# Splitting layer 2's k, r, v and LoRA weights during layer 1, and mixing block 0's operands twice

## The chip, the cores and the metric

The kernel runs on 1 core of one Trainium2 chip. The metric is the device time of one execution in microseconds (us). A profile of one execution shows what every engine did: TensorE (PE in the rows, PEld for its weight loads), VectorE (DVE), ScalarE (ACT), GpSimd (POOL), SyncE (SP, whose queue issues nearly all DMAs), and the 16 DMA engines.

## The reference

A trunk of four layers works on 256 context tokens and 1024 image tokens of width 1024, in float32. Layers 0 and 3 are RG-LRU mixers, layer 1 is an mLSTM mixer, layer 2 an RWKV-7 mixer. Cut to what matters here:

```python
# layer 1, mLSTM: 8 heads, q and k of 128, v and z of 256 columns a head
q, k, v, z, g = jnp.split(h @ w_in, splits, axis=-1)
# a recurrence over chunks, in both directions; then
out = (norm(hsum) * norm_g * silu(z)) @ w_out

# layer 2, RWKV-7: every projection has an operand of its own, mixed with the shifted tokens
xs = h[None] + (shifted - h)[None] * mu[:, None, None, :]        # r, k, v, z, w, a
r, k, v, z = einsum('gbtd,gde->gbte', xs[:4], w_rkvz)
w_pre = w0 + tanh(xs[4] @ w1) @ w2                               # LoRA of rank 64, two directions
a = sigmoid(a0 + (xs[5] @ a1) @ a2)                              # LoRA of rank 64, two directions
# then a recurrence over the tokens, forwards and backwards, for 16 heads
```

## The kernel before

Matrix products are done in three passes: weight and operand are each split into a rounded high part and the low part that remains, and high x high, high x low and low x high are added up (`mm3`, L107). So each weight is loaded raw, its high part is a cast, and its low part a subtraction.

**How instructions get their order.** Outside layer 2's scan the builder orders each engine's instructions by readiness in program order of priority. A tile of a pool gets one of the pool's buffers (their number is given for each name) once an earlier tile has been let go. `issue_after(x)` puts the instructions of x's engine that are made inside it behind x.

**Layer 1** (`mlstm`, L604) runs eight heads. Each head makes, in program order, q and k (three chunks of tokens each, `proj`), v (ten chunks, L650 to L652), the gate matrices E and Q for both directions, the products q k (L671), and then a loop of ten steps, in each step both directions (L678 to L711): the numerator (L689, L691), a normalisation by its last column (L693 to L695), the weighted keys on GpSimd (L703), the outer product (L705) and the new state on DVE (L83, from L710). Behind the loop come z0 and z1 (L714), the group norm and the output. Steps 1 to 6 also contain `ahead(1)`, one portion of the modulation parameters of layers 2 and 3, which DVE computes from loaded rows (`mw`, L230 and L232).

All weights of layer 1 come through `weight` (L96): the load at L101 on SP, the cast at L103 on DVE, the low part at L88 on GpSimd. Its tiles `wraw`, `whi` and `wlo` of 128x1024 come from the pool `wt`, which has two buffers for each name (L59).

**Layer 2** (`rwkv_scan`, L793) works on five blocks of 256 tokens, in the groups G0 = block 0, G1 = blocks 1 and 4, G2 = blocks 2 and 3. `stream` (L959) runs a list of projections: pieces of weights of 128x512 are loaded raw (`load`, at most two), split (`split`, cast on ACT at L986, low part on GpSimd, or on DVE in the first part) and, but for the two LoRA projections, written to memory in two parts (L992), so that later groups load the parts alone (L979, at most three pairs of buffers). `mixed` (L846) makes a projection's operand from h: a scaling on ACT, a shifted multiply-add on DVE, the high part on ACT, the low part on GpSimd or DVE. The first list is

```python
group(G0, (4, 5) + krv, half), group(G0, krv, rest, True), group(G1, (4, 5) + krv), ...
```

(4 and 5 are the LoRA projections, `krv` is k, r, v; `half` and `rest` are the first and the last four column tiles.) In the first group of G0 the operands of k, r and v are also written to memory (L897) and in the second they are read back (`again`, L903). The list's first 120 units run alone, up to r of the first group; the rest is dealt out between the instructions of the scan, whose order on each compute engine is the written one. The scan's first recurrence matmul (L1411) runs at 2143.8 us.

Of the kernel before, what the change touches and what calls it, by code (L numbers as in the profile page):

```python
# [10 lines left out]
F32 = mybir.dt.float32  # L11
# [19 lines left out]
class Net:  # L31
    def __init__(self, ctx, tc, aps):
        self.tc, self.nc, self.ctx = tc, tc.nc, ctx
        self.a = aps
        nc = self.nc
        pool = lambda name, bufs, **k: ctx.enter_context(tc.tile_pool(name=name, bufs=bufs, **k))
        self.const = pool("const", 1)
        self.sm = pool("sm", 1)
        self.base = ExitStack()
        self.open_base()  # L40
        c = self.const
        self.ones = c.tile([128, 128], F32, name="ones")
        nc.gpsimd.memset(self.ones, 1.0)
        self.ident = c.tile([128, 128], F32, name="ident")
        nc.gpsimd.affine_select(
            out=self.ident, in_=self.ones, pattern=[[-1, 128]], compare_op=ALU.is_equal,
            fill=0.0, base=0, channel_multiplier=1,
        )
        self.mhalf = c.tile([128, 16], F32, name="mhalf")
        nc.gpsimd.memset(self.mhalf, -0.5)  # L50
        self.vecs = c.tile([128, aps["vecs"].shape[1]], F32, name="vecs")
        nc.sync.dma_start(out=self.vecs, in_=aps["vecs"])
        self.spill = {}
        self.last = None

    def open_base(self):
# [547 lines left out]
    def mlstm(self, l, hs):  # L604
        nc = self.nc
# [3 lines left out]
        with ExitStack() as es:  # L609
# [6 lines left out]
            bc = lambda t: t.unsqueeze(2).to_broadcast([128, 10, 128])  # L616
            order = (tuple(range(10)), (1, 0) + tuple(range(9, 1, -1)))
            groups = ((0, 2), (2, 4), (6, 4))
            gof = {c: gi for gi, (a, n) in enumerate(groups) for c in range(a, a + n)}
            for h in range(8):  # L620
                E, Q = [], []
                w = self.weight(self.a["mlstm_w_q"][h], 8)
# [4 lines left out]
                w = self.weight(self.a["mlstm_w_k"][h], 8)  # L627
# [16 lines left out]
                for c in range(10):  # L644
                    ps = self.pm.tile([128, 512], F32, tag="pm", name="pm")[:, 0:256]
                    t = slice(c * 128, (c + 1) * 128)
# [7 lines left out]
                for d in (0, 1):  # L654
                    e = self.w(n=T, name="E")
# [11 lines left out]
                for gi, (a, n) in enumerate(groups):  # L667
                    ps = self.pa.tile([128, 512], F32, tag="pa", name="pa")
                    for i in range(n):
                        t = slice((a + i) * 128, (a + i + 1) * 128)  # L670
                        mm(ps[:, i * 128:(i + 1) * 128], kT[:, t], qT[:, t], start=True, stop=True)  # L671
                    for d in (0, 1):
                        p = E[d][:, a * 128:(a + n) * 128]
# [4 lines left out]
                for i in range(10):  # L678
                    for d in (0, 1):
                        if d and 0 < i < 7:  # L680
                            self.ahead(1)
                        c = order[d][i]
                        t = slice(c * 128, (c + 1) * 128)
                        gi = gof[c]
# [28 lines left out]
                for j in (0, 1):  # L713
                    w = self.weight(self.a["mlstm_w_z"][2 * h + j], 8)  # L714
# [15 lines left out]
                for a, n in groups:  # L730
                    for j in (0, 1):
# [6 lines left out]
                        self.stt(V, y[:, 0:n * 128], ps[:, 0:n * 128], ng[:, 2 * h + j:2 * h + j + 1], zs[j][:, s], ALU.mult, ALU.mult)  # L738
                        nc.sync.dma_start(out=yd[2 * h + j][:, s], in_=y[:, 0:n * 128])
            self.ahead(96)  # L740
        return yd

    def rwkv(self, l):
        hd = self.dram("r7h", (8, 128, T))
# [45 lines left out]
    def rwkv_scan(self, es, hd, zd, yd, xd):  # L792
# [46 lines left out]
        def parts(k, n):  # L839

            if n > 256 or k % 2 == 0:
                held[0] = tile_("xh", [128, 512], F32R, 8), tile_("xl", [128, 512], F32R, 8)
            o = 256 * (k % 2) if n == 256 else 0
            return [t[:, o:o + n] for t in held[0]]

        def mixed(g, k, blks, xs):  # L846
# [43 lines left out]
            S.copy(out=hi[:, 0:n], in_=t[:, 0:n])  # L890
            yield
            self.lo(V if early and k % 2 else G, lo[:, 0:n], t[:, 0:n], hi[:, 0:n])
            if g < 3 and blks == (0,):
                if k == 0:
                    xsp[g, blks] = [self.dram(f"r7x{g}_{blks[0]}_{j}", (2, 128, n)) for j in range(8)]
                for j, x in enumerate((hi, lo)):
                    nc.sync.dma_start(out=xsp[g, blks][k][j], in_=x.bitcast(F32))  # L897

        def again(g, k, blks, xs):

            xs[k] = parts(k, 256 * len(blks))
            for j, x in enumerate(xs[k]):
                nc.sync.dma_start(out=x.bitcast(F32), in_=xsp[g, blks][k][j])  # L903
            yield

        def drain(*gens):
            for g in gens:
# [46 lines left out]
                    done(c, acc[c])  # L954
            return job, [(name + (k,), w_ap[:, k * 512:k * 512 + 512]) for k in range(8)], 1, steps, 6

        wsp, xsp = {}, {}

        def stream(passes):  # L959

# [21 lines left out]
            def split():  # L982
                name, raw = raws.pop(0)
                hi, lo = pair()
                ready.append(((hi, lo), g))
                S.copy(out=hi, in_=raw)  # L986
                yield
                self.lo(V if early else G, lo, raw, hi)
                if name[0] != "l1":
                    d = self.dram("r7s" + "_".join(map(str, name)), (2, 128, 512))  # L990
                    for j, t in enumerate((hi, lo)):
                        nc.sync.dma_start(out=d[j], in_=t.bitcast(F32))  # L992
                    wsp[name] = d

            def start(gen):
                if gen is not None and next(gen, 0) is None:
# [42 lines left out]
                ready.pop(0)  # L1039
            drain(*work)  # L1040

        def group(blks, what, es=range(8), kept=False):
            n = 256 * len(blks)
            for g in what:
                job = Job(blks, [lambda xs, g=g, k=k, f=again if kept else mixed: f(g, k, blks, xs) for k in range(8)])
                if g >= 4:
                    def done(ps, g=g):
                        t = tile_("po", [128, 512], bufs=3)
# [447 lines left out]
        for k in range(8):  # L1496
# [2 lines left out]
        half, rest = range(4), range(4, 8)  # L1499
        krv = (1, 0, 2)  # L1500
        first = stream(itertools.chain(
            group(G0, (4, 5) + krv, half), group(G0, krv, rest, True), group(G1, (4, 5) + krv), group(G2, (4, 5) + krv),
            *(group(g, (3,)) for g in (G0, G1, G2)), output(G0, range(8), self.xsrc)))

        n = 120
# [220 lines left out]
```

## Time and profile before

| | us |
|---|---|
| median of 3 runs | 4512.19 |
| lowest and highest | 4493.22, 4515.55 |
| the profiled execution | 4495.78 |
| its span, first to last instruction | 4493.2 |

By stages of the profiled execution: layer 1's heads lie from about 690 to 1640 us, the first weight load of layer 2 is at 1912.9, the first matmul of its scan at 2143.8 and the last at 3875.8. In the rows a line can be that of a helper: L88 and L83 are the helpers for two-operand and three-operand instructions, so the names of the tiles tell more. A landing is the time from the issue of a DMA to its end.

### The profile page before, as it was taken

To read this page: it belongs to the slowest core of one execution; us is meant where nothing else is said; L and a number is where in the kernel's file an instruction comes from. 1 tells how busy PE (TensorE), PEld (TensorE's weight loads), DVE (VectorE), ACT (ScalarE), POOL (GpSimd) and SP (SyncE) were. 2 spreads that over 40 slices of the span, in tenths; PEclk is the share of its full clock that TensorE was granted. 3 is DMA by queue.
4 is the path that set the end of the run, shared out by engine and by line. 5 is a ranking of instruction groups with operands and counts; after the bars stand their busy time and mean duration, and the time that the engine had idled before them with its cause. 6 is when DMAs were issued, how large, how long until landed. Compare 5 with 4: busy or idle time off the path is not lost. (4 is left out here: it accounts for less than half of the span.)

```text
span 4493.2 us, 113560 instructions
## 1 busy us (share of the span) xinstructions
PE 3909.5 (87%) x47428; PEld 3173.9 (71%) x47428; DVE 2738.5 (61%) x5032; ACT 1960.7 (44%) x4103; POOL 2024.7 (45%) x1867
## 2 busy tenths in 40 slices
PE   5999898999999979857898799888888878779978
PEld 3677777888889868745676576666666766557766
DVE  4477746445555562444667666566688777467884
ACT  4577513222222220244544555455444544267760
POOL 2466623333333342125544533444455755347662
PEclk9999998999999989877999899988989879889999
DMA  5311422222222242388445645655344645411132
GB/s 210 121 47 51 151 86 71 88 92 92 92 88 91 88 163 65 118 297 275 147 145 172 195 162 163 208 153 163 111 127 134 208 129 156 155 60 54 52 114 81
DMA packets 355072, 581.10 MB, mean 129 GB/s; under 512 B 59232, under 2 KB 197472, under 8 KB 354432
## 3 DMA queue, kind: packets, MB, share of 16 engines
q1 hardware_dynamic: 354560, 573.85, 39.2%
q8 instruction: 373, 6.11, 0.6%
q14 instruction: 139, 1.14, 0.1%
HBM read 434.60 MB, written 139.10 MB: 128 GB/s over the span
## 5 line engine op out<-in xcount | busy, mean ns | idle before, releaser
L88 POOL TENSOR_TENSOR wlo<-wraw,whi 128x512 fp32r<-128x512 f32 (+3 forms) x260 | 483.6, 1861 | 752.5 <-DVE whi L103 375.0
L113 PE MATMUL pm<-hlo,whi 128*128 128x512 f32 (+1 forms) x1648 | 614.9, 373 | 10.0 <-DVE hlo L83 10.0
L114 PE MATMUL pm<-hhi,wlo 128*128 128x512 f32 (+1 forms) x1648 | 605.2, 370 | 11.8 <-POOL wlo L88 11.8
L112 PE MATMUL pm<-hhi,whi 128*128 128x512 f32 (+1 forms) x1648 | 612.0, 372 | 0.6 <-ACT hhi L290 0.6
L112 PE MATMUL pz<-xh,whi 128*128 128x512 f32 (+1 forms) x784 | 362.4, 463 | 27.4 <-DMA wraw<-in_r_l 17.4
L114 PEld LDWEIGHTS pm<-hhi,wlo 128*128 128x128 f32 x1648 | 312.5, 190 | 64.9 <-POOL wlo L88 15.2
L113 PEld LDWEIGHTS pm<-hlo,whi 128*128 128x128 f32 x1648 | 312.7, 190 | 63.8 <-DVE hlo L83 11.4
L112 PEld LDWEIGHTS pm<-hhi,whi 128*128 128x128 f32 x1648 | 313.3, 190 | 54.0 <-issue 1.7
L112 PE MATMUL pm<-yhi,whi 128*128 128x512 f32 (+1 forms) x816 | 302.9, 375 | 51.5 <-DVE x L83 28.2
L114 PE MATMUL pz<-xh,wlo 128*128 128x512 f32 (+1 forms) x784 | 302.8, 386 | 23.5 <-POOL wlo L88 23.2
L113 PE MATMUL pm<-ylo,whi 128*128 128x512 f32 (+1 forms) x816 | 303.6, 373 | 4.4 <-DVE ylo L88 2.5
L113 PE MATMUL pz<-xl,whi 128*128 128x512 f32 (+1 forms) x784 | 303.2, 387 | 2.0 <-POOL xl L88 1.0
L114 PE MATMUL pm<-yhi,wlo 128*128 128x512 f32 (+1 forms) x816 | 298.5, 373 | 4.0 <-POOL wlo L88 4.0
L88 POOL TENSOR_TENSOR t<-t,kin 128x256 f32<-128x256 f32 x88 | 82.4, 936 | 375.2 <-DVE t L1210 341.2
L103 DVE CAST whi<-wraw 128x1024 fp32r<-128x1024 f32 (+4 forms) x129 | 94.5, 733 | 257.4 <-PE pm L652 149.7
L83 DVE SCALAR_TENSOR_TENSOR x<-pm,mod,x 128x512 f32<-128x512 f32 (+1 forms) x208 | 136.5, 665 | 183.3 <-PE pm L114 165.8
L88 POOL TENSOR_TENSOR O<-DG,lev 128x256 f32<-128x256 f32 x200 | 160.4, 810 | 177.2 <-issue 117.7
L88 POOL TENSOR_TENSOR xl<-mx,xh 128x512 fp32r<-128x512 f32 (+1 forms) x146 | 178.5, 1232 | 130.0 <-ACT xh L890 85.8
L112 PEld LDWEIGHTS pm<-yhi,whi 128*128 128x128 f32 x816 | 156.1, 192 | 85.2 <-DVE x L83 31.5
L112 PEld LDWEIGHTS pz<-xh,whi 128*128 128x128 f32 x784 | 164.7, 210 | 68.4 <-ACT whi L986 27.5
L703 POOL TENSOR_SCALAR kw<-kt,tkwgt 128x128 f32<-128x128 f32 x144 | 105.3, 734 | 233.3 <-PE pa L705 188.9
L83 DVE SCALAR_TENSOR_TENSOR uf<-us,vecs,uf 128x1283 f32<-128x1283 f32 x60 | 158.5, 2641 | 82.8 <-ACT uf L411 80.3
(345 smaller groups left out, 10429.7 us busy)
## 6 DMA issues: line engine op xcount, KB each, us to landing
kin<-r7krk SPq DMA_DIRECT2D x72, 384.0 KB, 3.8
mw<-in_mod_w SPq DMA_DIRECT2D x48, 512.0 KB, 7.6
mw<-in_mod_w SPq DMA_DIRECT2D x96, 256.0 KB, 2.6
wlo<-r7sw SPq DMA_DIRECT2D x96, 256.0 KB, 3.0
whi<-r7sw SPq DMA_DIRECT2D x96, 256.0 KB, 2.7
wraw<-in_lru_w_in SPq DMA_DIRECT2D x40, 512.0 KB, 3.5
UZ<-r7v SPq DMA_DIRECT2D x160, 128.0 KB, 3.3
x<-x SPq DMA_DIRECT2D x28, 640.0 KB, 6.0
```

What stands on the lines that cost most here:

```text
L83: i = eng.scalar_tensor_tensor(out=out, in0=in0, scalar=scalar, in1=in1, op0=op0, op1=op1, **k)
L88: eng.tensor_tensor(out=out, in0=a, in1=b, op=op)
L103: (cast or nc.vector.tensor_copy)(out=hi, in_=raw)
L112: mm(out, w[0][:, c], x[0][:, a:a + b], start=first, stop=False)
L113: mm(out, w[0][:, c], x[1][:, a:a + b], start=False, stop=False)
L114: mm(out, w[1][:, c], x[0][:, a:a + b], start=False, stop=last)
L703: G.tensor_scalar(out=kw, in0=kt[:, t], scalar1=gt["wgt"][:, c, d, h:h + 1], scalar2=None, op0=ALU.mult)
```

## The change

While layer 1 runs, a generator `keep` takes the two LoRA weights, the k and r weights and the v weights of layer 2 in 26 tiles of 128x1024, splits each with `weight`, and writes the parts to memory in pieces of 128x512, under the names that `stream` uses. Its portions stand in the step loop: in the first two heads in steps 1, 3, 4 and 6, in the others in steps 1, 3 and 5, each with its DVE instruction behind the last state update. `stream` starts with these pieces as known ones, so it loads their parts and splits only z's and the output's weights. Block 0's operands of k, r and v are no longer written and read back; the second group of G0 mixes them again from h.

```diff
+            keep = self.keep()
...
                         if d and 0 < i < 7:
                             self.ahead(1)
+                        if d and i in ((1, 3, 4, 6) if h < 2 else (1, 3, 5)):
+                            with self.tc.issue_after(self.last.ins):
+                                next(keep, 0)
...
+    def keep(self):
+        nc = self.nc
+        for j, ap in [(("l1", 4 + g), self.a["r7_l1"][g]) for g in (0, 1)] + \
+                [(("w", g, e), self.a["r7_w"][g, e]) for h in (0, 4) for g in (1, 0) for e in range(h, h + 4)] + \
+                [(("v", h, 2 * k), self.a["r7_wv"][h][:, k * 1024:(k + 1) * 1024]) for h in (0, 1) for k in range(4)]:
+            hi, lo = self.weight(ap, 8)
+            for i in (0, 1):
+                name = (j[0], j[1], j[2] + i) if j[0] == "v" else j + (4 * i,)
+                d = self.dram("r7s" + "_".join(map(str, name)), (2, 128, 512))
+                for p, t in enumerate((hi, lo)):
+                    nc.sync.dma_start(out=d[p], in_=t[:, i * 512:(i + 1) * 512].bitcast(F32))
+                self.kept[name] = d
+            yield 1
...
             self.lo(V if early and k % 2 else G, lo[:, 0:n], t[:, 0:n], hi[:, 0:n])
-            if g < 3 and blks == (0,):
-                if k == 0:
-                    xsp[g, blks] = [self.dram(f"r7x{g}_{blks[0]}_{j}", (2, 128, n)) for j in range(8)]
-                for j, x in enumerate((hi, lo)):
-                    nc.sync.dma_start(out=xsp[g, blks][k][j], in_=x.bitcast(F32))
-
-        def again(g, k, blks, xs):
...
-        wsp, xsp = {}, {}
+        wsp = self.kept
...
-                if name[0] != "l1":
-                    d = self.dram("r7s" + "_".join(map(str, name)), (2, 128, 512))
-                    for j, t in enumerate((hi, lo)):
-                        nc.sync.dma_start(out=d[j], in_=t.bitcast(F32))
-                    wsp[name] = d
+                d = self.dram("r7s" + "_".join(map(str, name)), (2, 128, 512))
+                for j, t in enumerate((hi, lo)):
+                    nc.sync.dma_start(out=d[j], in_=t.bitcast(F32))
+                wsp[name] = d
...
-            group(G0, (4, 5) + krv, half), group(G0, krv, rest, True), group(G1, (4, 5) + krv), group(G2, (4, 5) + krv),
+            group(G0, (4, 5) + krv, half), group(G0, krv, rest), group(G1, (4, 5) + krv), group(G2, (4, 5) + krv),
```

## Rows read from the trace of the kernel before

**Rows 1.** The page: busy time of each engine, share of the span, instructions.
```profile
PE 3909.5 (87%) x47428; PEld 3173.9 (71%) x47428; DVE 2738.5 (61%) x5032; ACT 1960.7 (44%) x4103; POOL 2024.7 (45%) x1867
```

**Rows 2.** Busy time by stretch: start:end, length, each engine busy (instructions), PE clock, DMA share, GB/s.
```profile
1001.40:1064.20 62.80, 62.80 (x305) 53.60 (x304) 43.63 (x140) 13.52 (x40) 16.61 (x17) 1.00 0.27 84
1064.20:1115.40 51.20, 51.20 (x389) 48.86 (x388) 14.38 (x30) 15.45 (x31) 22.15 (x14) 1.00 0.28 99
1115.40:1560.00 444.60, 444.60 (x2664) 398.26 (x2663) 229.11 (x668) 114.39 (x280) 152.67 (x123) 1.00 0.28 93
1912.00:1992.00 80.00, 47.17 (x254) 42.96 (x254) 47.61 (x96) 46.26 (x113) 19.74 (x26) 0.75 0.86 287
1992.00:2144.00 152.00, 106.91 (x1030) 81.89 (x1030) 54.93 (x93) 62.24 (x131) 87.17 (x81) 0.76 0.86 278
```

**Rows 3.** Timeline of TensorE in layer 1, one recurrence step: start, length, instruction.
```profile
1008.83 0.59 PE L689 MATMUL pa<-vt,E 128*128 128x257 f32 x2
1009.26 0.60 PE L691 MATMUL pa<-st,Q 128*128 128x257 f32 x2
1009.69 0.60 PE L705 MATMUL pa<-vt,kw 128*128 128x257 f32 x2
```

**Rows 4.** Timeline of SP's queue in the same head of layer 1: weight loads.
```profile
1001.28 0.33 SPq L101 DMA_DIRECT2D wraw<-in_mlstm_w_q  x1
...
1029.53 0.38 SPq L101 DMA_DIRECT2D wraw<-in_mlstm_w_v  x1
...
1071.93 0.33 SPq L101 DMA_DIRECT2D wraw<-in_mlstm_w_z  x1
```

**Rows 5.** Timeline of DVE, same head: state update, first direction, steps 3, 4, 5.
```profile
1022.97 0.48 DVE L83 SCALAR_TENSOR_TENSOR st<-st,dec,pa 128x257 f32<-128x257 f32 x1
...
1030.60 0.47 DVE L83 SCALAR_TENSOR_TENSOR st<-st,dec,pa 128x257 f32<-128x257 f32 x1
...
1035.82 0.48 DVE L83 SCALAR_TENSOR_TENSOR st<-st,dec,pa 128x257 f32<-128x257 f32 x1
```

**Rows 6.** Busy time of the engines from the recurrence's start to step 3.
```profile
1001.40:1023.00 21.60, 21.60 (x105) 18.38 (x104) 15.19 (x51) 6.15 (x16) 6.17 (x7) 1.00 0.29 86
```

**Rows 7.** The raw weight tiles in layer 1: ns min/median/max, first and last start, forms.
```profile
L103 DVE CAST whi<-wraw x48: 284/694/2314, 642.4 to 1540.1; 128x1024 fp32r<-128x1024 f32 x46, 128x384 fp32r<-128x384 f32 x1, 128x256 fp32r<-128x256 f32 x1
...
L88 POOL TENSOR_TENSOR wlo<-wraw,whi x48: 737/2384/2414, 642.9 to 1540.9; 128x1024 fp32r<-128x1024 f32 x46, 128x384 fp32r<-128x384 f32 x1, 128x256 fp32r<-128x256 f32 x1
...
DMA to landing us min/median/max: 3.3/4.1/8.4
```

**Rows 8.** The loads of z's weights in layer 1.
```profile
DMA to landing us min/median/max: 3.4/7.0/8.4
```

**Rows 9.** Timeline of all engines in layer 1, around one low part on GpSimd.
```profile
1024.09 0.69 DVE L232 SCALAR_TENSOR_TENSOR mw<-mw,scr 128x512 f32<-128x512 f32 x1
...
1026.15 2.37 POOL L88 TENSOR_TENSOR wlo<-wraw,whi 128x1024 fp32r<-128x1024 f32 x1 [2.52 <-PE pa L691]
...
1026.26 2.81 DVE L232 SCALAR_TENSOR_TENSOR mw<-mw,scr 128x512 f32<-128x512 f32 x1
```

**Rows 10.** DMA issues, front of layer 2: xcount, KB each, median us to landing.
```profile
DMA packets 51277, 65.17 MB, mean 281 GB/s; under 512 B 9471, under 2 KB 31161, under 8 KB 51257
...
wraw<-in_r_w SPq DMA_DIRECT2D x32, 256.0 KB, 3.7
...
r7sw<-whi SPq DMA_DIRECT2D x32, 256.0 KB, 4.2
...
xh<-r7x SPq DMA_DIRECT2D x24, 128.0 KB, 4.0
```

**Rows 11.** Groups on ACT, front of layer 2: busy us, mean ns, idle before.
```profile
L986 ACT CAST whi<-wraw 128x512 fp32r<-128x512 f32 x55 | 33.8, 614 | 69.4 <-DMA wraw<-in_r_w 28.0 <-DMA wraw<-in_r_wv 19.3 <-PE pz L113 8.3
...
L868 ACT ACTIVATE mx<-X,omu 128x256 f32<-128x256 f32 x40 | 18.7, 503 | 8.5 <-DMA X<-r7h 6.2 <-POOL xl L88 2.0 <-DVE xl L88 0.2
```

**Rows 12.** Waits of TensorE, front of layer 2: total us, times, longest.
```profile
PE pz L1116 <- ACT kq L1110: 34.5, 8, 8.3
```

More of the change, by code (lines that the diff above doesn't have):

```diff
@@ L52, in __init__ @@
         nc.sync.dma_start(out=self.vecs, in_=aps["vecs"])
-        self.spill = {}
+        self.spill, self.kept = {}, {}
         self.last = None
@@ L740, in mlstm @@
             self.ahead(96)
-        return yd
+            for _ in keep:
+                pass
+        return yd
+    def keep(self):
[11 more added lines that the diff above has]
+            yield 1
     def rwkv(self, l):
@@ L892, in mixed @@
             self.lo(V if early and k % 2 else G, lo[:, 0:n], t[:, 0:n], hi[:, 0:n])
-            if g < 3 and blks == (0,):
-                if k == 0:
-                    xsp[g, blks] = [self.dram(f"r7x{g}_{blks[0]}_{j}", (2, 128, n)) for j in range(8)]
-                for j, x in enumerate((hi, lo)):
-                    nc.sync.dma_start(out=xsp[g, blks][k][j], in_=x.bitcast(F32))
-        def again(g, k, blks, xs):
[L901 to L904, printed above, removed]
         def drain(*gens):
@@ L1040, in stream, with group @@
             drain(*work)
-        def group(blks, what, es=range(8), kept=False):
+        def group(blks, what, es=range(8)):
             n = 256 * len(blks)
             for g in what:
-                job = Job(blks, [lambda xs, g=g, k=k, f=again if kept else mixed: f(g, k, blks, xs) for k in range(8)])
+                job = Job(blks, [lambda xs, g=g, k=k: mixed(g, k, blks, xs) for k in range(8)])
                 if g >= 4:
```

## The prediction

> **What bounds the kernel now.** I read the page's first lines, then the busy time by stretch, then inside two stretches the matmul groups, the issues on SP's queue and the steps on DVE. TensorE is busy for 87% of the span [rows 1], but this hides two very different stages. In layer 1 TensorE has no idle time at all: 62.80 of 62.80 us, 51.20 of 51.20 and 444.60 of 444.60, at a granted clock of 1.00, with the DMA engines at 0.27 to 0.28 [rows 2]. At the front of layer 2, from 1912 to 2144, it is busy 47.17 of 80.00 and 106.91 of 152.00 us at a clock of 0.75 and 0.76, and the DMA engines are at 0.86 in both [rows 2]. So layer 1 pays for whatever takes matmuls from TensorE, and the front of layer 2 pays for bytes. The change moves work from the second to the first.
>
> A layer 1 head takes 114.0 us (62.8 + 51.2). Its recurrence, ten steps in each direction, lies in the 62.8 us [rows 2]. Its own matmuls are short: three kinds in a row start 0.43 us apart [rows 3], and there are 20 + 18 + 18 of them by the code (the first step has no state to read), so 24 us, 2.4 a step. The other 39 us of TensorE are projections with weights already on the chip: z of this head, then q of the next. This filler is why TensorE never waits for the recurrence, whose pace DVE and the hand-overs between engines set.
>
> **Part 1: what the kept weights do to layer 1.** The code gives all weights of layer 1 one pool of two buffers each for the raw tile, the high and the low part, and keep() takes its tiles from that pool. SP's queue shows that buffers are taken in program order, as soon as they are free: q at 1001.28, v at 1029.53, z at 1071.93, the last 43 us before its matmuls, which begin with the next recurrence at 1115.4 [rows 2, 4]. In the code the new tiles stand in the recurrence, after v and ahead of z. Their loads wait for nothing but a buffer, so they come first. Their casts are tied behind the recurrence's update of step 1, 3, 5 (for the first two heads 1, 3, 4, 6). So z0 gets its raw buffer only when the kept tile of step 3 has been split (of step 4 in the first two heads), and z1 that of the one after. Until then TensorE has only the recurrence's 2.4 us a step.
>
> How long: the recurrence of the head shown starts at 1001.4; the update of step 3 in the first direction runs at 1022.97, that is +21.6 us [rows 5]. Without z beside it this can be earlier. DVE was busy 15.19 us up to there [rows 6]; without z's two evictions (an estimate: 0.7 each, as the 0.69 us instructions of their size [rows 9]), and with the first kept tile's cast and its delay (2.8 us, below), that makes +16.6. I take +20, as the DVE work is most but not all of it. Then four 0.69 us instructions of the modulation (2.8 us [rows 9], 3.1 with their read-outs), the cast 0.69 and the low part 2.38 us [rows 7]: the raw buffer is free at +26. The load lands 4.1 us later (3.3 to 8.4 [rows 7]; z's own 7.0 [rows 8]), cast and a place in DVE's order take 1.5: z0's first matmul at +32. A step takes 6.4 us here (1022.97 to 1035.82 for two [rows 5]), so 5 steps, 12 us of matmuls, are done by then: TensorE idles 20 us a head. Ends: the kept tile before the modulation at +16.6, landing in 3.3: +24, 10 us done, 14 us idle; step 3 at +21.6, delays of 2.1 us twice, landing in 7.0: +41, 14.5 us done, 26 us idle. In the first two heads step 4 is 6 to 8 us later (1030.60 [rows 5]), 2.4 us more done: +3.5 idle. Nothing gives it back, as the rest of the head is 51.20 of 51.20 us busy [rows 2]. Eight heads: 8 x 20 + 2 x 3.5 = **+167 us** (119 to 215).
>
> The rest of part 1 costs little by itself. 26 kept tiles are 26 casts at 0.69 (18 us of DVE), 26 low parts at 2.38 (62 us of GpSimd) and 26 x 1.57 MB (512 KB read, four writes of 256 KB) = 41 MB over some 920 us, 44 GB/s beside the stage's 84 to 99, with DMA at 0.27 [rows 2]. DVE has 43.6 of 62.8 us in use in the recurrence [rows 2], GpSimd 16.6. SP's queue takes 26 x 5 issues of 0.33 us; the writes wait there for their cast and low part, and the modulation's loads queue behind them, which is inside the upper end. The cover for all of this is the filler that part 1 takes away.
>
> One thing more lengthens the steps: a low part on GpSimd from 1026.15 for 2.37 us has beside it a modulation instruction on DVE that takes 2.81 us instead of 0.69, and the DVE one ends 0.55 us after it [rows 9]. So each kept tile can hold DVE for 2.1 us; that is the delay above. The Trainium skill, SBUF — State Buffer, section "Who interferes with whom", says that a DVE instruction with two SBUF inputs and a GpSimd instruction that reads SBUF share a port pair, and that the later one waits for the whole of the earlier. The trace agrees with this (2.81 against 0.69 us). By that rule all 26 low parts could hit, 26 x 2.1 = 55 us of DVE; without it the sum would lose some 2 us a head. It speaks against putting this work beside the recurrence.
>
> **Part 2: the front of layer 2.** From 1912 to 2144 the core moves 65.17 MB at 281 GB/s [rows 10]. All 52 weight pieces of the first pass (4 LoRA, 32 of k and r, 16 of v) are loaded raw, 256 KB, and 48 are written back as two parts; 24 operand tiles are written and read back as two parts of 128 KB [rows 10]. Before: 13.6 + 25.2 + 12.6 = 51.4 MB. After: 52 x 512 KB = 27.3 MB, and 24 reads of 128 KB of h for the second mixing, 3.1 MB: 30.4. So 21.0 MB fewer, at 281 GB/s **-75 us**. TensorE's own busy time in this stretch is 154 of 232 us, so 78 is the most while its clock stays at 0.75; where both rise it can be 100. The low end, 55, is where loads in three buffers or the start of the scan set the pace: a pair must be read whole before its first matmul.
>
> ACT loses 52 casts at 0.614 (32 us) and gets 48 instructions for the second mixing, at most 0.503 each (24 us) [rows 11]; it is at 46.26 of 80.00 and 62.24 of 152.00 [rows 2], so it does not become the bound. GpSimd and DVE lose 52 low parts of 512 columns and get 24 of 256, and DVE 24 shifts: less for both. SP issues 52 + 96 + 96 fewer and 104 + 24 more. Later passes read the LoRA weights instead of splitting them: a few microseconds, taken as zero, since TensorE is the fuller engine there. The scan's order is written out, so an earlier start moves its end one for one.
>
> **Sum.** 4495.8 (the profiled execution; span 4493.2) + 167 - 75 = 4588. The ends: +119 - 100 = +19 and +215 - 55 = +160, so 4515 to 4656. The median of the runs shown is 4512.2, 16 above the profiled one; the forecast is on the profiled one's scale.
>
> **Rivals.** *Faster: TensorE keeps its filler.* If z's loads get buffers ahead of the kept ones, or other matmuls are put into the hole, part 1 costs nearly nothing and the time is 4496 - 75 = 4421. For it: the builder orders instructions by readiness, as filler between steps shows; against: every load of [rows 4] is in program order, and q, k and v of the next head stand behind z in the same buffers. It decides for faster where z0's first matmul comes before about +15 us in the step loop, as 75 us over eight heads is 9.4 us idle a head. *No change: half the hole.* If without filler the steps run at twice the pace, the kept tile of step 3 comes at about +11 and z0 at +21, idle 10 us a head: 4496 + 84 - 75 = 4505. For it: TensorE would answer each step at once; against: DVE's 15.19 us [rows 6], of which z's evictions are the small part. *Slower still: part 2 gives little.* If the first pass is held by latency (TensorE waits 34.5 us of it for the tile of the norm of k, a chain of hand-overs [rows 12]), it gives 25: 4496 + 167 - 25 = 4638. That kept weights are not found under their names, and split again, I exclude: the names in keep() are those that stream() asks for; it would be 4663.
>
> **How the numbers follow.** Forecast 0.53, slower still 0.12, no change 0.15, faster 0.20. A measurement of this kernel tells about 0.5% (22 us) from no change. The forecast's low tail and the rival give same 0.15; slower is 0.65, faster 0.20. The forecast's own range is 4515 to 4656; the range given reaches down to 4440 to take in no change and the weak end of the faster case, and ends at 4655, the forecast's own upper end.
>
> **What would show it.** In layer 1: raw loads in the order v, kept, kept, kept, z, and TensorE idle some 20 us in the first half of each recurrence, ended by DVE's cast or GpSimd's low part of z; a head of 130 to 137 us instead of 114.0; perhaps a clock below 1.00 in the hole. In layer 2: some 44 MB from the first weight load to the first chain matmul, in some 157 us instead of 232. Wrong would be: heads of 114 to 118 us, or z loaded before the kept tiles.

## The result and the profile after

The changed kernel takes 4567.66 us (median of 4 runs, 4552.67 to 4570.89), the kernel before 4503.92 (median of 4, 4493.22 to 4515.55) beside it: a ratio of 1.0133, 95% interval 1.0107 to 1.0158. It is slower by 1.3%, as forecast in sign (4588, range 4440 to 4655). Both of the prediction's terms, however, came out about half as large as they were put, and because they have opposite signs their errors partly cancelled: that the total lies near the forecast is in part luck. The profiled executions, 4495.78 before and 4552.67 after, split like this (the scan's row ends with its last output product, 4 us behind the last recurrence matmul):

| stage | before | after | difference | forecast |
|---|---|---|---|---|
| up to layer 1's output (first write of h for layer 2) | 1885.3 | 1979.2 | +93.9 | +167 |
| from there to the first load of h | 23.0 | 22.8 | -0.1 | 0 |
| front of layer 2: first load of h to first scan matmul | 235.5 | 200.6 | -34.9 | -75 |
| scan | 1736.1 | 1737.5 | +1.4 | 0 |
| rest | 613.3 | 610.7 | -2.6 | 0 |
| span | 4493.2 | 4551.0 | +57.8 | +92 |

The engines' busy line of the page of after answers [rows 1]. It tells little, as it did before: TensorE's share falls by one point.

```profile
PE 3934.0 (86%) x47428; PEld 3170.1 (70%) x47428; DVE 2803.2 (62%) x5061; ACT 1942.4 (43%) x4091; POOL 2079.8 (46%) x1878
```

The busy time by stretch tells more. Columns as in [rows 2]; the first two lines are the third head of layer 1, cut 1.8 to 2.2 us ahead of its recurrence as there, the third is four heads, the fourth the whole front of layer 2.

```profile
1030.50:1093.30 62.80, 53.98 (x246) 42.91 (x245) 54.79 (x158) 12.62 (x41) 29.75 (x21) 0.97 0.45 151
1093.30:1157.60 64.30, 64.30 (x448) 59.72 (x447) 11.87 (x13) 15.83 (x32) 20.25 (x13) 1.00 0.24 86
1157.60:1669.60 512.00, 477.07 (x2762) 414.90 (x2762) 265.67 (x681) 114.10 (x284) 199.02 (x136) 0.97 0.34 118
2002.10:2202.70 200.60, 136.16 (x1283) 113.44 (x1283) 98.44 (x190) 97.74 (x237) 79.60 (x97) 0.81 0.73 230
```

The recurrence's stretch, full before, has 8.82 us without a matmul and a clock of 0.97, and DVE is busy 54.79 of its 62.80 us (43.63 before). The front is shorter, at a DMA share of 0.73 instead of 0.85.

**The hole, read instruction by instruction.** SP's queue of the same head, weight loads, answers [rows 4]: the second and third kept tile (named `in_r_w`; the first was loaded at 990.41), and only then z0 and z1.

```profile
1005.44 0.33 SPq L101 DMA_DIRECT2D wraw<-in_r_w  x1
...
1043.62 0.42 SPq L101 DMA_DIRECT2D wraw<-in_r_w  x1
...
1053.96 0.42 SPq L101 DMA_DIRECT2D wraw<-in_mlstm_w_z  x1
...
1062.76 0.42 SPq L101 DMA_DIRECT2D wraw<-in_mlstm_w_z  x1
```

The timeline of all engines in that head shows what z0 waited for.

```profile
1036.40 0.48 DVE L83 SCALAR_TENSOR_TENSOR st<-st,dec,pa 128x257 f32<-128x257 f32 x1
...
1037.41 0.69 DVE L103 CAST whi<-wraw 128x1024 fp32r<-128x1024 f32 x1
...
1038.20 0.68 DVE L232 SCALAR_TENSOR_TENSOR mw<-mw,scr 128x512 f32<-128x512 f32 x1
...
1038.54 2.54 POOL L88 TENSOR_TENSOR wlo<-wraw,whi 128x1024 fp32r<-128x1024 f32 x1
...
1038.81 2.82 DVE L232 SCALAR_TENSOR_TENSOR junk<-mw,scr 128x512 f32<-128x512 f32 x1
...
1047.64 0.46 DVE L83 SCALAR_TENSOR_TENSOR st<-st,dec,pa 128x257 f32<-128x257 f32 x1
...
1048.02 0.68 DVE L103 CAST whi<-wraw 128x1024 fp32r<-128x1024 f32 x1
...
1048.79 2.72 POOL L88 TENSOR_TENSOR wlo<-wraw,whi 128x1024 fp32r<-128x1024 f32 x1 [0.80 <-DVE whi L103]
...
1056.01 0.47 DVE L83 SCALAR_TENSOR_TENSOR st<-st,dec,pa 128x257 f32<-128x257 f32 x1
...
1060.94 0.68 DVE L103 CAST whi<-wraw 128x1024 fp32r<-128x1024 f32 x1
...
1062.35 0.46 DVE L83 SCALAR_TENSOR_TENSOR st<-st,dec,pa 128x257 f32<-128x257 f32 x1
...
1062.35 0.58 PE L112 MATMUL pm<-hhi,whi 128*128 128x512 f32 x1
```

The cast at 1037.41 is the first kept tile's, the one at 1048.02 the second's, right behind the update it is tied to. The second's low part ends at 1051.51, z0's load is issued into that buffer at 1053.96, z0 is cast at 1060.94 (the third kept tile's cast, at 1056.40, is not shown), and its first matmul runs at 1062.35, 31.9 us after the stretch began and 29.7 after the recurrence's first matmul. Until then TensorE has only the recurrence.

The waits of TensorE in the front of after (us in total, times, longest) answer [rows 12].

```profile
PE pz L1124 <- ACT kq L1118: 25.7, 6, 6.8
PE pz L112 <- DMA whi<-r7sl: 16.3, 1, 16.3
PE px L1191 <- DVE bon L1312: 5.9, 1, 5.9
PE pz L112 <- DMA whi<-r7sw: 4.7, 5, 1.8
```

The longest is still the norm of k (34.5 us before, 25.7 now). It makes three tiles, a square, a broadcast factor and the product, one after the other in a single buffer (`kq`), and TensorE's sum over the squares (L1124) waits until ACT has written the square there (L1118), which needs the buffer free. But for the stage's first load, 16.3 us, waits for the weights are small.

### The profile page after: what moved, and what is told of

It is laid out like the page before. It is cut to its first block, busy times and chain, and to the rows that moved or that the text cites. A ratio compares the mean times of both kernels' runs of the same rounds, so it can differ in the third digit from the quotient of the medians.

```text
span 4551.0 us, 113706 instructions
## 1 busy us (share of the span) xinstructions
PE 3934.0 (86%) x47428; PEld 3170.1 (70%) x47428; DVE 2803.2 (62%) x5061; ACT 1942.4 (43%) x4091; POOL 2079.8 (46%) x1878
## 4 chain that ended last, share of the span: by engine, by line
PE 31%; DVE 9%; issue 6%; POOL 4%; ACT 4%; DMA 4%; SPq 1%; POOLq 0%; DVEq 0%; ACTq 0%
PE pm L112 4%; PE pm L113 4%; PE pm L114 4%; PE pz L112 3%; PE pz L114 2%; PE pz L113 2%; PE pi L1341 2%; PE pi L1351 2%; DMA hp<-r7h 1%; DVE mx L83 1%; PE px L1261 1%; PE pc L1419 1%; PE pc L1438 1%; PE pc L1433 1%; POOL O L88 1%
## 5 line engine op out<-in xcount | busy, mean ns | idle before, releaser
L88 POOL TENSOR_TENSOR wlo<-wraw,whi 128x1024 fp32r<-128x1024 f32 (+3 forms) x247 | 513.9, 2081 | 848.5 <-DVE whi L103 410.8
L113 PE MATMUL pm<-hlo,whi 128*128 128x512 f32 (+1 forms) x1648 | 604.7, 367 | 10.0 <-DVE hlo L83 10.0
L112 PE MATMUL pz<-xh,whi 128*128 128x512 f32 (+1 forms) x784 | 358.5, 458 | 23.2 <-DMA whi<-r7sl 16.3
L88 POOL TENSOR_TENSOR xl<-mx,xh 128x512 fp32r<-128x512 f32 (+1 forms) x170 | 197.6, 1172 | 159.4 <-ACT xh L911 115.8
L88 POOL TENSOR_TENSOR O<-DG,lev 128x256 f32<-128x256 f32 x200 | 160.2, 809 | 188.5 <-issue 117.8
L707 POOL TENSOR_SCALAR kw<-kt,tkwgt 128x128 f32<-128x128 f32 x144 | 118.9, 831 | 193.2 <-PE pa L709 184.3
```

The lines of the kernel that those rows point to most:

```text
L88: eng.tensor_tensor(out=out, in0=a, in1=b, op=op)
L112: mm(out, w[0][:, c], x[0][:, a:a + b], start=first, stop=False)
L113: mm(out, w[0][:, c], x[1][:, a:a + b], start=False, stop=False)
L707: G.tensor_scalar(out=kw, in0=kt[:, t], scalar1=gt["wgt"][:, c, d, h:h + 1], scalar2=None, op0=ALU.mult)
```

## The experiments

All times below are medians against the kernel before on the same chip. Stages come from the profiled execution, one for each kernel. Its scan took between 1732.0 and 1763.7 us over all these kernels, with no relation to the edits that one profile each would show, so layer 1 and the front are read by themselves, and the verdict on a whole kernel comes from the ratio. "Heads" are the distances between the starts of the recurrences of layer 1 (before: 115.7, then 114.0 to 114.1).

### Layer 1: is it the shared buffers, their order, or the tie?

**Own buffers.** The kept tiles get two buffers of another pool instead of `wt`'s; the low part is written over the raw tile.

```diff
-            hi, lo = self.weight(ap, 8)
+            raw, hi = self.w(n=1024, name="kraw"), self.w(F32R, 1024, "khi")
+            nc.sync.dma_start(out=raw, in_=ap)
+            nc.vector.tensor_copy(out=hi, in_=raw)
+            lo = raw.bitcast(F32R)
+            self.lo(nc.gpsimd, lo, raw, hi)
```

> The change with one thing else: a kept tile takes two buffers of the big pool of 27 (raw with the low part written over it, and high) and none of the two-buffer weight pool; its place, its tie to the steps, its cast, its low part and its writes stay. Theory A (the kept tiles hold the two weight buffers, so z cannot be loaded and TensorE has no filler): z's loads come right behind v's again, a layer 1 head takes 114 to 118 us instead of the change's 127 to 130, and the time is 75 to 95 us below the change: 4473 to 4493, ratio to the kernel before 0.993 to 0.998. Theory B (the added DVE and GpSimd work beside the steps lengthens them): heads stay at 125 to 130 us and the time at 4555 to 4575, ratio 1.011 to 1.016.

Measured: 4492.99 us, ratio 0.9964 (0.9946 to 0.9982); heads of 121.7, 125.2, then 117.6, where after has 130.4, 130.1, then 127.1 to 128.2 (theory A). z0's matmuls start with the recurrence again. The same casts, low parts, loads and writes are there, tied to the same steps: so the hole is the buffers, not the added work, and the work keeps some 3.6 us a head.

**Own order.** The kept portions stand behind z's loads instead of in the steps, in the shared buffers, without a tie.

```diff
-                        if d and i in ((1, 3, 4, 6) if h < 2 else (1, 3, 5)):
-                            with self.tc.issue_after(self.last.ins):
-                                next(keep, 0)
...
+                for _ in range(4 if h < 2 else 3):
+                    next(keep, 0)
```

> The change with the kept tiles moved in program order from the steps to behind z's two loads, without the tie; same pool of two buffers, same work. Theory A: the hole at the head of the recurrence goes, and a shorter one comes behind z1, where q of the next head now waits for the kept tiles' buffers: heads of 118 to 124 us, time 4505 to 4540, ratio 1.000 to 1.008. Theory B (the work itself): heads stay at 125 to 130 us, ratio 1.011 to 1.016.

Measured: 4480.22 us, ratio 0.9932 (0.9911 to 0.9954); heads of 117.2, 120.4, then 116.6 to 117.4. The hole goes, as theory A says, but both heads and ratio (1.000 to 1.008) were expected higher: the second hole, behind z1, did not come. The weight loads on SP's queue in this kernel: z's for the recurrence that starts at 1126 are issued 30 to 45 us ahead of it.

```profile
1010.61 0.33 SPq L101 DMA_DIRECT2D wraw<-in_r_w  x1
...
1038.60 0.44 SPq L101 DMA_DIRECT2D wraw<-in_r_w  x1
...
1081.12 0.33 SPq L101 DMA_DIRECT2D wraw<-in_mlstm_w_z  x1
...
1096.38 0.33 SPq L101 DMA_DIRECT2D wraw<-in_mlstm_w_z  x1
```

**No tie.** Kept tiles ahead of z as in the change, but all portions at step 1 and without the tie to an update.

```diff
-                        if d and i in ((1, 3, 4, 6) if h < 2 else (1, 3, 5)):
-                            with self.tc.issue_after(self.last.ins):
+                        if d and i == 1:
+                            for _ in range(4 if h < 2 else 3):
```

> The change with the kept tiles still ahead of z in the two-buffer pool, but all of a head's portions at step 1 and without the tie behind the state update. It asks whether the length of the hole is the time for which the kept tiles hold the buffers. In the change z0's first matmul comes 32 us into the recurrence. If the hold time decides: casts run as soon as v's buffers are free, z0 comes at about +18 to +22 us, 10 us of the recurrence done by then, so a head of 121 to 125 us, time 4515 to 4545, ratio 1.001 to 1.008. If the steps' pace decides (DVE is back to back in the hole, whatever the place of the casts): heads stay at 127 to 130 us, ratio 1.011 to 1.016.

Measured: 4521.02 us, ratio 1.0016 (0.9998 to 1.0035), no difference that can be told; heads of 125.2, 126.5, then 122.3 to 123.1. From the third head on z0's first matmul comes 13 to 15 us after the recurrence's first (29 to 30 in after). So the tie, with the later steps it goes with, makes over half of the hole, and 5 of the 14 us a head. The other 9 stay; some 3 of them are there with the kept tiles behind z too (own order), so the place ahead of z makes about 6. The prediction's point of decision was z0 at about +15 us, with 75 us won in the front. With the 38 us that this front wins (197.2 against 235.5), z0 at +13 to +15 gives a whole time that can't be told from before; by the profiled stages it still costs 25 us (63.2 more up to layer 1's output, 38.3 less in the front).

**Low parts on DVE.** As the change, but the kept low parts are DVE's.

```diff
...
-            hi, lo = self.weight(ap, 8)
+            hi, lo = self.weight(ap, 8, low=nc.vector)
```

> The change with one thing else: the kept tiles' low parts are made on DVE instead of GpSimd. On GpSimd one takes 2.4 to 2.7 us, and a DVE instruction beside it was seen at 2.8 instead of 0.69 us; on DVE it should take about 1.4 (0.69 for half the columns in layer 2). If the two engines hold each other up: DVE is blocked 26 x 2.1 us less and works 26 x 1.4 more, and z's buffers come free 1 us sooner for each kept tile: heads 1 to 4 us shorter (124 to 127), time 10 to 30 us below the change, ratio 1.006 to 1.011. If the contention costs nothing on the path: heads 127 to 130, since DVE is back to back there and gets more work, ratio 1.013 to 1.017.

Measured: 4537.15 us, ratio 1.0054 (1.0033 to 1.0075), 0.8% under the changed kernel; heads of 126.6, 127.5, then 123.4 to 124.1; z0's first matmul at +23.1 from the recurrence's first. The engine that looked full, DVE, gets more work, and the heads get 4 us shorter: the raw buffers come free sooner (a low part takes 1.2 us on DVE against 2.7 on GpSimd, medians), and DVE is no longer held up beside them. How much each of the two gives, this run does not separate.

### The front: bytes, the norm of k, or the splits?

**Three buffers for the norm of k**, in the changed kernel, for block 0.

```diff
-            sq = tile_("kq", [128, 512], bufs=1)
+            tq = ("kq", "sq", "vt") if blks == (0,) else ("kq",) * 3
+            sq = tile_(tq[0], [128, 512], bufs=1)
...
-            rb = tile_("kq", [128, 512], bufs=1)
+            rb = tile_(tq[1], [128, 512], bufs=1)
...
-            rn = tile_("kq", [128, 512], bufs=1)[:, 0:n]
+            rn = tile_(tq[2], [128, 512], bufs=1)[:, 0:n]
```

> The change with the three tiles of the norm of k (square, broadcast, result) in three buffers instead of one, for block 0 only. It asks why the front of layer 2 fell by 35 us (235.5 to 200.6, from the first load of h to the first scan matmul) and not by 75. Theory C (the norm's one buffer holds the stream, as TensorE's longest wait there, 25.7 us, says): front 175 to 188 us, time 4542 to 4556, ratio 1.009. Theory D (that wait only covers others: loads of the pairs, the scan's own hand-overs in their written order): front 195 to 202 us, time within 6 us of the change, ratio 1.013.

Measured: 4548.74 us, ratio 1.007 (1.0042 to 1.0099); front 180.1 us, 20.5 shorter (theory C). The wait for the norm of k is gone from the head of the list.

**The second half undone.** The changed kernel with block 0's operands written and read back as before.

```diff
...
-            group(G0, (4, 5) + krv, half), group(G0, krv, rest), ...
+            group(G0, (4, 5) + krv, half), group(G0, krv, rest, True), ...
```

> The change with its second half undone: block 0's operands of k, r and v are written to memory and read back again, the kept weights stay. 12.6 MB of writes and reads come back and 3.1 MB of reads of h go. If the front of layer 2 is still set by bytes: 9.5 MB at 231 GB/s, 41 us longer, 4600 to 4612, ratio 1.022. If it is set by hand-overs: within 10 us of the change, ratio 1.011 to 1.016. If the second mixing itself is on the path (the chain of the changed kernel names its loads of h): 8 to 20 us shorter, ratio 1.009 to 1.011.

Measured: 4569.68 us, ratio 1.0136 (1.0113 to 1.0159), the changed kernel's own; front 201.4 us with 55.67 MB instead of 46.22. So 9.4 MB, 34 us at the rate of [rows 10], are worth nothing here (as expected if hand-overs set the front).

**Both repairs.** Kept portions behind z's loads (own order, above) and three buffers for the norm of k.

```diff
...
-                                next(keep, 0)
...
+                for _ in range(4 if h < 2 else 3):
+                    next(keep, 0)
...
-            sq = tile_("kq", [128, 512], bufs=1)
+            tq = ("kq", "sq", "vt") if blks == (0,) else ("kq",) * 3
+            sq = tile_(tq[0], [128, 512], bufs=1)
...
```

> The kept tiles behind z (as in the second experiment) and three buffers for the norm of k of block 0 (as in the fourth), together. Alone they gave a ratio of 0.9932, and 19 us off the change. If the stages add up, as layer 1 and the front of layer 2 lie behind one another: heads of 117 us, front of 176 to 184 us, 4455 to 4470, ratio 0.986 to 0.991. If the scan gives the earlier start back (it is dealt out in a written order): front 180 but the scan longer by as much, ratio 0.991 to 0.995.

Measured: 4463.56 us, ratio 0.9882 (0.9851 to 0.9912): faster than both kernels, and as expected if the stages add up. Heads of 117.8, 120.1, then 116.7 to 117.3; front 179.9.

**The kernel before with three buffers for the norm of k**, and nothing else.

```diff
-            sq = tile_("kq", [128, 512], bufs=1)
+            tq = ("kq", "sq", "vt") if blks == (0,) else ("kq",) * 3
+            sq = tile_(tq[0], [128, 512], bufs=1)
...
```

> The kernel before, with one edit: for block 0 the three tiles of the norm of k (sq, rb, rn) lie in three buffers instead of one. Theory A: in the kernel before the front of layer 2 (235.5 us from the first weight load's issue to the first scan matmul) is bound by the 65 MB it moves, so the edit does nothing there: front 228 to 238 us, ratio 0.998 to 1.001. Theory B: the front waits for hand-overs before the change too, the norm of k among them: front 205 to 222 us (the edit took 20 us off the front of the changed kernel), ratio 0.994 to 0.997. Layer 1 is the same as before under both (heads of 114 us).

Measured: 4505.77 us, ratio 0.9979 (0.9962 to 0.9996); front 235.6 us against 235.5. The front is not shorter, which is theory A's number; where the 0.2% lies is open, as no stage before the scan moved. Yet the norm's wait fell. TensorE's waits in the front of before, the norm's 34.5 us [rows 12] and then:

```profile
PE pz L947 <- ACT whi L986: 12.4, 12, 2.5
PE pz L114 <- POOL wlo L88: 9.0, 4, 7.3
PE pz L112 <- ACT whi L986: 6.0, 4, 2.9
PE pz L951 <- POOL wlo L88: 4.3, 8, 2.9
```

and with the three buffers:

```profile
PE pz L112 <- ACT whi L986: 18.6, 12, 3.9
PE pz L947 <- ACT whi L986: 16.8, 10, 3.8
PE pz L114 <- POOL wlo L88: 12.6, 9, 7.3
PE pz L1117 <- ACT kq L1111: 8.5, 6, 2.5
```

The time moved from the norm to the casts of the weights (18.4 us before, 35.4 here). That bytes alone set this front, as theory A says, the next run refutes.

**The second half alone**, in the kernel before: nothing kept, block 0's operands mixed twice.

```diff
...
-                for j, x in enumerate((hi, lo)):
-                    nc.sync.dma_start(out=xsp[g, blks][k][j], in_=x.bitcast(F32))
...
-            group(G0, (4, 5) + krv, half), group(G0, krv, rest, True), ...
+            group(G0, (4, 5) + krv, half), group(G0, krv, rest), ...
```

> The kernel before with the second half of the change alone: nothing is kept during layer 1, block 0's operands of k, r and v are mixed a second time instead of written and read back. Theory A: the front of the kernel before (235.5 us, 65.17 MB) is bound by bytes; 9.5 MB fewer at 281 GB/s are 34 us: front 198 to 208 us, heads of 114 us, ratio 0.991 to 0.995. Theory B: what holds it is the splitting of the weights itself (casts and low parts, loads in few buffers) or the norm of k: front 225 to 238 us, ratio 0.997 to 1.001.

Measured: 4514.46 us, ratio 1.0015 (0.9995 to 1.0035); front 237.0. This is theory B. The edit also adds the second mixing, whose price no run takes apart from that of the bytes. The stretch, then, is at a lower DMA share and as long:

```profile
1910.80:2147.90 237.10, 156.36 (x1283) 125.32 (x1283) 119.65 (x211) 126.40 (x292) 124.77 (x131) 0.75 0.74 237
```

**The same with three buffers for the norm of k.**

```diff
...
-            sq = tile_("kq", [128, 512], bufs=1)
+            tq = ("kq", "sq", "vt") if blks == (0,) else ("kq",) * 3
+            sq = tile_(tq[0], [128, 512], bufs=1)
...
-            group(G0, (4, 5) + krv, half), group(G0, krv, rest, True), ...
+            group(G0, (4, 5) + krv, half), group(G0, krv, rest), ...
```

> The kernel before with the second half of the change alone and three buffers for the norm of k in block 0; nothing is kept during layer 1. Theory A: bytes set this front too (55.7 MB at 281 GB/s, 198 us), so the buffers add nothing: front within 5 us of the run without them. Theory B: with fewer bytes the norm of k becomes the bound, as in the changed kernel: front 10 to 20 us shorter than the run without them, ratio lower by 0.002 to 0.005.

Measured: 4496.61 us, ratio 0.997 (0.9951 to 0.9988); front 225.0, 12 us below the run without the buffers (theory B). What TensorE waits for most there are the splits:

```profile
PE pz L114 <- POOL wlo L88: 17.0, 9, 7.2
PE pz L112 <- DMA hp<-r7h: 16.7, 1, 16.7
PE pz L1112 <- ACT kq L1106: 11.1, 4, 4.8
PE pz L942 <- ACT whi L981: 9.7, 10, 2.2
PE pz L112 <- ACT whi L981: 5.2, 4, 2.4
PE pz L946 <- POOL wlo L88: 4.9, 5, 2.4
```

Low parts and casts end 36.8 us of waits (17.0 + 9.7 + 5.2 + 4.9), and the one load of 16.7 us is the stage's first, which every kernel here waits for in some form.

**Both repairs with the second half undone**: 9.4 MB more, where no norm and no split stands in the way.

```diff
...
-            group(G0, (4, 5) + krv, half), group(G0, krv, rest), ...
+            group(G0, (4, 5) + krv, half), group(G0, krv, rest, True), ...
```

> The changed kernel with the kept portions behind z's loads, no tie, three buffers for the norm of k in block 0 (front of 179.9 us in that kernel), and here block 0's operands written and read back as before the change, 9.5 MB more in the front. Theory A: without the wait for the norm of k the bytes set the front again: 55 to 57 MB at the 281 GB/s of the kernel before are 196 to 203 us, so a front of 192 to 203, some 16 us above, and a ratio of 0.990 to 0.994. Theory B: the front is held by hand-overs alone whatever it moves: front 178 to 184 us, ratio 0.987 to 0.990.

Measured: 4471.41 us, ratio 0.9924 (0.9898 to 0.995); front 194.5, 14.6 us longer (theory A). Its waits, the first load of 17.0 us apart, are now weights from memory, at a DMA share of 0.90:

```profile
PE pz L112 <- DMA wlo<-r7sl: 17.0, 1, 17.0
PE pz L112 <- DMA whi<-r7sw: 12.4, 8, 2.6
PE pz L114 <- DMA wlo<-r7sw: 12.2, 13, 4.0
PE pz L967 <- DMA whi<-r7sv: 8.6, 8, 2.1
```

The eight fronts together (MB moved in the front, us):

| weights | operands of block 0 | MB | one buffer for the norm | three buffers |
|---|---|---|---|---|
| split in the front | written, read back | 65.7 | 235.5 (before) | 235.6 |
| split in the front | mixed twice | 56.2 | 237.0 | 225.0 |
| kept | written, read back | 55.7 | 201.4 | 194.5 |
| kept | mixed twice | 46.2 | 200.6 (after) | 179.9, 180.1 |

Other kernels here repeat two of these cells: kept and mixed twice took 197.2 to 202.9 us with one buffer, 177.7 to 180.1 with three, so a difference of some 5 us is not to be read. Down a column: keeping the weights is worth 34 to 45 us in every pair. That is not the bytes: the second and the third row move nearly the same, and differ by 36 and 30 us (their other difference, the second mixing, costs nothing in the kept rows). Fewer operand bytes, for a second mixing, are worth nothing (+1.5, -0.8) while the norm has one buffer, 10.6 and 14.6 us when it has three. Three buffers are worth nothing or 7 us with the bytes there, 12 and 21 us without them (the 7 us are a kernel with own order against one without). So splits, bytes and norm lie close behind each other, and each repair shows only where the others are out of the way.

### What was left of layer 1's cost

**Both repairs, and the kept low parts on DVE.**

```diff
...
-            hi, lo = self.weight(ap, 8)
+            hi, lo = self.weight(ap, 8, low=nc.vector)
```

> The changed kernel with the kept portions behind z's loads, no tie to a step, three buffers for the norm of k in block 0 (as in the run before it of that kind, heads of 117 to 120 us, ratio 0.988), and here the kept low parts on DVE instead of GpSimd. Theory A: the 3 us a head that are left over the kernel before come from kept low parts on GpSimd holding DVE's instructions up: heads of 115 to 116 us, ratio 0.985 to 0.988. Theory B: they come from elsewhere (SP's queue, or the buffers of q, k and v of the next head taken by kept tiles): heads of 117 us or more, ratio 0.988 to 0.990.

Measured: 4464.51 us, ratio 0.9886 (0.9855 to 0.9918); heads of 117.5, 116.2, then 114.0 to 114.1. In layer 1 that is theory A, and better than it put it: from the third head on nothing of the 3 us is left (the first two, with four kept tiles each, keep some 2). The whole time doesn't show the 11 us that layer 1 is shorter than with both repairs alone (1891.5 against 1902.5), but the intervals are 0.6% wide, 28 us. Five heads, third to eighth recurrence, first of the kernel with both repairs:

```profile
1012.50:1597.80 585.30, 574.67 (x3451) 511.87 (x3450) 322.57 (x853) 143.02 (x355) 235.22 (x171) 1.00 0.39 129
```

and of the kernel with the low parts on DVE as well:

```profile
1008.60:1578.80 570.20, 570.20 (x3451) 512.68 (x3450) 323.44 (x868) 145.16 (x355) 194.22 (x156) 1.00 0.40 132
```

TensorE is full again, with all kept work beside it. DVE has 15 instructions more, low parts of 1215 ns median, 18 us together, and yet nearly the same busy time (323.44 against 322.57 us). The modulation's instructions, 60 in each, show why, with both repairs and then with the low parts on DVE as well:

```profile
L232 DVE SCALAR_TENSOR_TENSOR mw<-mw,scr 128x512 f32<-128x512 f32 x60 | 73.6, 1227 | 0.7
```

```profile
L232 DVE SCALAR_TENSOR_TENSOR mw<-mw,scr 128x512 f32<-128x512 f32 x60 | 41.5, 691 | 0.5
```

The moved low parts had held these up by 32 us. DVE's instructions on `r` and `E` became longer in the same step (18.7 us before it, 35.3 after), for a reason that is not shown; that is why the busy time did not fall.

## Why the prediction was right in sign, and where its sizes failed

**What bounds each stage.** For layer 1 this held: TensorE was full, and nothing gave the hole back except in the last head. For the front it failed. "The front of layer 2 pays for bytes" was read from a DMA share of 0.86 [rows 2]; taking 9.4 MB off it, for a second mixing, left it at 237.0 us. The Trainium skill, Perfetto Trace Analysis, section "Identifying the Most-Contended Engine", says that the occupancy of 16 DMA engines is misleading as a measure of the bound. The runs here agree: 0.85 and 0.74 of DMA share gave 235.5 and 237.0 us.

**Part 1: +94 instead of +167.** The mechanism is as forecast: the order of loads, the tie, z0 behind the second kept tile, its first matmul at +31.9 against +32. That one agreement hides two errors that cancelled: the buffer was free sooner (+21.0 against +26, as the cast ran right behind the update, not behind the modulation, and the update came at +17.1 against +20), while z0 took longer from its issue to its cast (7.0 us, the figure of [rows 8], against 4.1 and 1.5), and its issue came 2.45 us after the buffer was free. Of the 31.9 us the first 2.2 lie ahead of the recurrence, where TensorE is full; the forecast counted its 1.8 us of them into the hole. The heads took 127 to 130 us, at the foot of the 130 to 137 forecast. Three terms were mis-sized:

- *What the recurrence gets done in the hole*: forecast 5 steps, 12 us of matmuls. Measured in the 29.7 us from the recurrence's first matmul to z0's: 78 records, two to a matmul, so 39 of the 56, which is 7 of the 10 steps, and 16.8 us at the 0.43 us of [rows 3]. In the same time the kernel before runs 54 records, 27 matmuls, 11.6 us. Without filler a step takes 4.2 us on the mean of these seven; the first direction's updates of steps 1 to 6 come 5.2 us apart (1036.40 to 1062.35), not the 6.4 read from [rows 5], where z's matmuls and evictions lay between. The rival "half the hole" said that steps would run at twice the pace; it had the right cause, with too much of it. So the hole costs 13 to 14 us a head, not 20. In five heads (1032.7 to 1671.8) TensorE has 43.75 us without a matmul, 38.7 of them waiting for a state update, as the first line of its waits says, and 25.25 us more of busy time for the same matmuls (595.35 against 570.10), as they overlap less and the clock is at 0.98 (added up one by one they take only 5 us more, 1162.8 against 1157.4): 69.0 us, 13.8 a head.

```profile
PE pa L709 <- DVE st L83: 38.7, 21, 3.7
PE pa L709 <- POOL kw L707: 3.2, 5, 0.6
```

- *The number of heads*: forecast 8; the last costs nothing. Before, TensorE was busy 34.70 of the 60 us behind that head's recurrence (1640 to 1700), where no next head's projections follow; after, 55.59 of 60: the late z fills that gap. From the last recurrence to the end of the layer it is 307.4 us against 312.0.
- *The first two heads*: forecast 3.5 us more each, measured +14.7 and +16.0 against 13.8 for the others.

Sum: 14.7 + 16.0 + five heads of 13.8, less 4.6 behind the last and 1.2 at the start, is 93.9.

**The delay by GpSimd's low parts** held in mechanism and was put too small in its place. The first kept low part has beside it a DVE instruction of 2.82 us, as [rows 9] had. The Trainium skill, SBUF — State Buffer, section "Who interferes with whom", has the rule of the shared port pair, and the trace agrees: 2.82 against 0.68 us. The prediction put "some 2 us a head" on it; moving the low parts to DVE took 4 us a head off the changed kernel, and the last 3 us a head off the repaired one.

**Part 2: -35 instead of -75.** The step that failed is "21.0 MB fewer, at 281 GB/s". The bytes did fall (65.7 to 46.2 MB, 19.4 against the 21.0 forecast), but the rate fell too, from 279 to 230 GB/s. The rival "part 2 gives little" named one of the holders, the norm of k, from [rows 12], and gave 25 us with a chance of 0.12; the measured 34.9 is nearer to it than to the forecast. It left out the other, the splits. Of the 34.9, 17.7 are TensorE's own busy time, 153.90 to 136.16 for the same matmuls, while its clock rose from 0.76 to 0.81 (means of its two levels, 1.2 and 2.4 GHz; before, TensorE had stood idle for 82 of the 235.5 us, after for 64 of 200.6). The clock is not all of it: with the second half undone the same matmuls took 142.74 us at 0.77. And what was won was won by keeping the weights, not by the bytes: the casts and low parts that ended 31.7 us of TensorE's waits before (12.4 + 9.0 + 6.0 + 4.3) are on after's list no more, and the second half of the change, the mixing, is worth nothing in it. Which part of the split work counts most (casts, low parts, raw loads in two buffers), no run separates. One row of the prediction already spoke for this: 34.5 us of waits on one buffer's hand-over are no sign of a byte bound alone.

**The rest.** The scan did start 34.9 us earlier relative to layer 1's end, and its length did not answer (+1.4). Kept weights were found under their names. The profiled execution lies 35 us under the forecast: -73 in layer 1, +40 in the front, -1 in the rest. The median is 15 us above the profiled execution, so it lies 20 us under.

## What to carry to other kernels

Before new tiles go through a pool that others use, write down in which order its buffers will be taken and which stalled tile then stands ahead of a load that the bottleneck needs: placed behind z's loads, the same work cost 3 us a head instead of 14, and with its low parts on another engine none from the third head on. A stage with a high DMA share and a long wait of the main engine on a single buffer can have several bounds close behind each other: undo them one at a time and together before putting a price on one, and don't take bytes over a rate for it. And when an engine loses its filler, what is left runs faster than it did among the filler, so a hole costs less than its length minus the work that the old pace would have got done in it.

## What the runs showed of the hardware

A subtraction of two 128x1024 float32 tiles took 1.2 us on DVE and 2.4 us on GpSimd, and on GpSimd it also held DVE up: 15 of them moved to DVE, 18 us in five heads, took the modulation's 60 instructions from 73.6 to 41.5 us, and DVE, with two other kinds 17 us longer (above), was busy for 0.9 us longer in all. The core moved 286 GB/s at a DMA share of 0.90 where bytes did show in the time, and 279 at 0.85 where fewer bytes did not: the share doesn't tell the two apart, the list of waits does (weights from memory at its top in the one, casts, low parts and the norm in the other). The Trainium skill, Perfetto Trace Analysis, section "Optimization Strategy", says that the same gap repeated on the engine that should be full can mean too few buffers for the next tile; the hole here is such a gap, eight times, and buffers of their own for the kept tiles closed it; so did another order in the same two buffers.
